# Turning a layer's output with VectorE and device memory instead of TensorE

## The chip, the cores and the metric

The kernel runs on one core of a Trainium2 chip. The core has a matrix engine (TensorE, PE in the profile), VectorE (DVE), ScalarE (ACT), GpSimd (POOL) and SyncE (SP), a scratch memory of 128 partitions (SBUF), an accumulator memory that the matrix engine writes (PSUM, banks of 512 float32 per partition), and 16 transfer engines (DMA) that are fed by the queues of SP, ACT and POOL. The metric is the time of one execution on the device in microseconds; lower is better. All times below are microseconds unless marked otherwise.

## The reference

Two layers, each with three parallel groups of heads on one input projection; then an output projection, a residual and a layer norm. One sequence of 256 positions with 2048 features, all float32.

```python
def layer_norm(x, g, b):
    mu = mean(x); var = mean((x - mu) ** 2)
    return (x - mu) * rsqrt(var + 1e-5) * g + b

def hybrid_layer(x, mem, w_in, ..., w_mem_kv, w_out, ln_g, ln_b):
    h = x @ w_in
    a_q, a_k, a_v, a_z, b_q, b_k, b_v, b_z, b_lr, m_q, m_z = split(h)
    y_a = chunk_band_attention(a_q, a_k, a_v, rel_table)
    y_b = rms_norm(gla_chunk_recurrence(b_q, b_k, b_v, log_sigmoid(b_lr @ gate_w + gate_b) / 16))
    mk, mv = split(mem @ w_mem_kv)
    y_m = memory_attention(m_q, mk, mv)
    y = concatenate([y_a * silu(a_z), y_b * silu(b_z), y_m * silu(m_z)])
    return layer_norm(sqrt(2) * x + y @ w_out, ln_g, ln_b)

for l in range(2):
    h = hybrid_layer(h, mem, w_in[l], ...)
```

## The kernel before

**Products.** Almost all time goes into products of activations with streamed weights. To keep float32 accuracy each operand is split into a high and a low part (`parts`, L114: ScalarE casts the high part, VectorE subtracts it for the low part), and three products are added: high x high, low x high, high x low. Weights come in pieces of 512 KB (`piece`, L128): SP loads a piece into a tile `raw`, ScalarE writes `wh`, VectorE writes `wl`. The pool of these tiles has four buffers of each (`wp`, L79), so the split of a piece waits until TensorE is done with the piece four before it. Two forms of product occur: `as_group` (L272) holds the activations still and streams the weights; `ws_group` (L254) holds the weights still and streams high and low activations side by side (`both`, 512 columns). A `ws_group` has two halves of four pieces; piece number q multiplies quarter q of the features, x[q].

**Between the layers.** The output of layer 0 lies in `res` with positions on partitions (two tiles t of 128 positions, 2048 features each). Layer 1 needs it with features on partitions: operands x[0] to x[3] (`xq`), each [128, 4, 2, 256], which is four blocks of 128 features, high and low part, 256 positions. `norm_between` (L627) normalises `res` in place: ScalarE takes column groups 0 and 2, VectorE 1 and 3. `transposed` (L574) then turns it: for each pair of feature blocks four 128x128 transposes on TensorE into a PSUM bank (L590), then ScalarE and VectorE scale one block each with the norm's gain and bias (L596, L598, per-partition values in `gT`, which L578 and L579 turn out of a row-wise copy), and `parts` splits the result into x. `restored` (L602) applies gain and bias to `res` itself, for the next residual.

**Order.** TensorE and SP run in the order in which the program is written (L49). ScalarE, VectorE and GpSimd are put in order by the scheduler, by data and priority (`tc.high_priority`); the order is fixed when the program is built, and each engine executes its own list in order. Small jobs are generators; `tick` (L52), called after each weight piece, advances one of them by a step, so that each `yield` places the following instructions behind one more piece. `transposed` is started behind group MV (values of the memory) and runs during group MK (keys of the memory, eight pieces); `finish(gens[:1])` (L779) completes it before the first product that reads x, group BQK (L783), which is again a `ws_group` of eight pieces.

**Buffers.** Operands x come from a pool of five (`opp`, L78): four hold the memory's operand during MV and MK, so that x[1] to x[3] take places that MK's second half frees piece by piece. The tag "qk" of pool `hd` has four buffers of 4 KB a partition; they hold q and k of the attention heads (L802, L837).

**GpSimd** computes almost nothing. It issues small loads (gate weights L303, norm vectors L649, L879) and fills constants (L358).

## Time and profile before

| what | value |
|---|---|
| median of 3 runs | 925.61 (925.45 to 925.86) |
| the profiled execution, whole time | 925.59 |
| its span in the profile | 923.8 |
| granted TensorE clock | 0.998 |
| busy: PE, DVE, ACT, POOL | 916.7, 587.9, 498.2, 21.8 |
| moved by transfers | 178.85 MB, mean 194 GB/s |
| group MK on TensorE | 479.38 to 505.54, with the transposes between its pieces |

The profile shows one execution. Its page gives busy times, the span in slices, the transfer queues, the chain of work that ended last, and groups of instructions. Beside the page the trace can be asked for a timeline of one engine, for groups of instructions in a stretch, and for busy times and transfer rates in chosen stretches. Start times count from the start of the span. A line such as `idle before <-releaser` names what ended an engine's wait.

### The profile page before, as it was taken

Reading aid. Unit: us, or ns where it says so; the run is one execution under the profiler, and the core shown is the slowest. Engines: PE = TensorE matmul, PEld = TensorE weight load, DVE = VectorE, ACT = ScalarE, POOL = GpSimd, SP = SyncE. Lnnn points to the kernel's source line nnn. Section 1 sums busy time; section 2 is a strip of 40 time slices with the busy share of each in tenths; the row PEclk is TensorE's granted clock in tenths of the full one; section 3 lists DMA queues with packets and bytes.
Section 4 is the critical chain, followed back from the end, with each engine's and each line's share of the span. In section 5 each row is a group of like instructions: output and inputs, shape, how many; then the busy total and the mean of one; then the engine's idle time right before and its main releaser. Section 6 shows DMA issues by size and latency. Waiting matters only on the chain.

```text
span 923.8 us, 14249 instructions
## 1 busy us (share of the span) xinstructions
PE 916.7 (99%) x5500; PEld 806.5 (87%) x5500; DVE 587.9 (64%) x812; ACT 498.2 (54%) x714; POOL 21.8 (2%) x49
## 2 busy tenths in 40 slices
PE   9999999999999999999999999999999999999997
PEld 7889998998888888888888899889888888888885
DVE  6764478665564666555587666975655555766566
ACT  6644485484454675433566445754744555754350
POOL 1000000000000000000000000000000000110000
PEclk9999999999999999999999999999999999999999
DMA  9955865546554566756675466546555544667652
GB/s 306 334 189 174 306 207 173 161 165 194 183 162 160 171 206 200 219 193 196 227 249 164 150 205 204 193 154 196 170 193 166 164 152 160 199 222 223 198 163 92
DMA packets 71253, 178.85 MB, mean 194 GB/s; under 512 B 7304, under 2 KB 31240, under 8 KB 70928
## 3 DMA queue, kind: packets, MB, share of 16 engines
q1 hardware_dynamic: 69120, 173.30, 57.1%
q0 software_dynamic: 1920, 4.36, 1.8%
q8 instruction: 43, 0.70, 0.3%
q10 hardware_dynamic: 144, 0.26, 0.1%
q14 instruction: 26, 0.21, 0.1%
HBM read 175.77 MB, written 2.10 MB: 193 GB/s over the span
## 4 chain that ended last, share of the span: by engine, by line
PE 98%; DMA 0%; DVE 0%; ACT 0%; SPq 0%; issue 0%
PE acc L93 89%; PE bk L93 8%; PE bk L526 1%; DMA raw<-w 0%; PE bk L561 0%; PE bk L590 0%; PE bk L494 0%; PE bk L393 0%; SPq L177 0%; ACT res L746 0%; ACT wh L116 0%; DVE stats L731 0%; PE bk L340 0%; DVE res L730 0%; DVE res L682 0%
## 5 line engine op out<-in xcount | busy, mean ns | idle before, releaser
L117 DVE TENSOR_TENSOR wl<-raw,wh 128x1024 fp32r<-128x1024 f32 (+3 forms) x321 | 370.0, 1154 | 255.9 <-ACT wh L116 254.9
L116 ACT CAST wh<-raw 128x1024 fp32r<-128x1024 f32 (+3 forms) x321 | 318.7, 994 | 329.9 <-PE acc L93 236.5
L93 PE MATMUL acc<-x,wh 128*128 128x512 f32 x1248 | 398.0, 400 | 0.1
L93 PE MATMUL acc<-wh,x 128*128 128x512 f32 (+2 forms) x1236 | 357.3, 370 | 0.1
L93 PEld LDWEIGHTS acc<-x,wl 128*128 128x128 f32 x1248 | 234.4, 188 | 55.3
L93 PEld LDWEIGHTS acc<-wh,x 128*128 128x128 f32 x1236 | 227.0, 188 | 27.9 <-ACT wh L116 0.6
L93 PE MATMUL acc<-x,wl 128*128 128x256 f32 x1248 | 246.0, 278 | 0.0
L93 PE MATMUL acc<-wl,x 128*128 128x512 f32 (+2 forms) x618 | 228.0, 369 | 0.0
L93 PEld LDWEIGHTS acc<-x,wh 128*128 128x128 f32 x1248 | 192.0, 189 | 1.9 <-ACT wh L116 0.4
L93 PEld LDWEIGHTS acc<-wl,x 128*128 128x128 f32 x618 | 116.0, 188 | 15.0 <-DVE wl L117 0.9
L518 ACT ACTIVATE sc<-sc,mx 128x128 f32<-128x128 f32 (+1 forms) x32 | 14.4, 450 | 20.3 <-DVE mx L516 20.3
L511 DVE SCALAR_TENSOR_TENSOR sc<-bk,bias 128x384 f32<-128x384 f32 x16 | 8.9, 554 | 12.7 <-PE bk L93 12.7
L382 ACT ACTIVATE sc<-sc 128x512 f32<-128x512 f32 x12 | 7.6, 633 | 12.5 <-DVE sc L380 12.5
L117 DVE TENSOR_TENSOR x<-sc,x 128x512 fp32r<-128x512 f32 x20 | 13.3, 684 | 0.7 <-ACT x L116 0.7
L116 ACT CAST x<-raw 128x1024 fp32r<-128x1024 f32 x5 | 5.3, 1053 | 15.3 <-DMA raw<-memT 12.7
L117 DVE TENSOR_TENSOR x<-res,x 128x512 fp32r<-128x512 f32 (+2 forms) x14 | 10.5, 765 | 4.2 <-ACT x L116 4.1
L93 PE MATMUL bk<-qk,qk 128*128 128x128 f32 (+1 forms) x64 | 13.1, 326 | 0.0
L117 DVE TENSOR_TENSOR x<-raw,x 128x1024 fp32r<-128x1024 f32 x5 | 6.1, 1225 | 10.9 <-ACT x L116 10.9
L93 PE MATMUL bk<-sc,asv 128*128 128x256 f32 (+1 forms) x64 | 13.0, 326 | 0.0
L262 DVE SCALAR_TENSOR_TENSOR sc<-acc,sc 128x512 f32<-128x512 f32 x19 | 12.9, 681 | 0.0
L116 ACT CAST x<-sc 128x512 fp32r<-128x512 f32 x20 | 11.8, 615 | 1.3 <-DVE sc L598 1.3
L623 DVE SCALAR_TENSOR_TENSOR res<-res,acc 128x512 f32<-128x512 f32 x15 | 9.7, 684 | 4.2 <-PE acc L93 4.2
(209 smaller groups left out, 567.8 us busy)
## 6 DMA issues: line engine op xcount, KB each, us to landing
raw<-w SPq DMA_DIRECT2D x214, 512.0 KB, 3.9
raw<-w SPq DMA_DIRECT2D x64, 388.0 KB, 3.3
raw<-w SPq DMA_DIRECT2D x83, 256.0 KB, 3.2
bias<-relw SPq DMA_DIRECT2D x16, 192.0 KB, 4.1
res<-xT SPq DMA_DIRECT2D x4, 512.0 KB, 5.0
res<-xn SPq DMA_DIRECT2D x1, 2048.0 KB, 8.2
raw<-memT SPq DMA_DIRECT2D x4, 512.0 KB, 4.3
res<-memT SPq DMA_DIRECT2D x6, 256.0 KB, 6.1
```

The costliest lines, as they stand in the source:

```text
L93: pe.matmul(o, l, r, start=start, stop=stop, skip_group_check=True)
L116: act.copy(hi, src)
L117: dve.tensor_tensor(lo, src, hi.bitcast(F32), op=ALU.subtract)
L262: dve.scalar_tensor_tensor(dst, a, scale, dst, op0=ALU.mult, op1=ALU.add)
L382: act.activation(dd, dd, AF.Abs)
L511: dve.scalar_tensor_tensor(s, pb[:, :384], SCALE, bias[h], op0=ALU.mult, op1=ALU.add)
L518: act.activation(s[:, own[t]], s[:, own[t]], AF.Exp, bias=mx[:, t:t + 1], accum_out=zs[:, t:t + 1])
L526: pe.transpose(pt[:, i * P:(i + 1) * P], s[:, i * P:(i + 1) * P], ident)
L623: dve.scalar_tensor_tensor(r, r, ALPHA, acc, op0=ALU.mult, op1=ALU.add)
```

## The change

TensorE no longer transposes `res`. VectorE turns it in blocks of 32x32 (`dve.transpose`): four instructions, one for each tile t of positions and each half c of a 128-feature block, write tiles `turned` with 32 features on the partitions of each 32-partition stripe. GpSimd writes them into a device-memory tile `blocks` in 16 transfers (64 rows of 2 KB each), which puts the stripes of positions side by side, and loads it again in four transfers of 512 KB (`raws`, 1024 rows of 512 bytes each), one for each quarter of the features. `raws` has features on partitions, eight stripes of 32 positions, and is scaled in place and split into x through a rearranged view. `turned` and `raws` use the four buffers of the tag "qk". The whole quarter q, its load too, is now issued at raised priority. The transfer of the turned blocks is placed over four steps of the generator, the four quarters over four more. A pool in device memory (`drm`) is added. The number of scalings and splits on ScalarE and VectorE stays the same.

```diff
+    drm = enter("drm", 3, space=bass.MemoryType.DRAM)
...
         pe.transpose(pt[:, :P], raw, ident)
         dve.tensor_copy(gT, pt[:, :32])
+        blocks = drm.tile([P, 8, 512], F32, name=nm("blocks"), tag="blocks", bufs=1)
+        turned = {}
+        for t in range(2):
+            for c in range(2):
+                turned[t, c] = hd.tile([P, 2, 16, 32], F32, name=nm("turn"), tag="qk", bufs=4)
+                dve.transpose(turned[t, c].rearrange("p b k j -> p k b j"),
+                              res[:, t].rearrange("p (k b j) -> p k b j", b=4, j=32)[:, :, 2 * c:2 * c + 2])
+        yield 2
+        for t in range(2):
+            for c in range(2):
+                for a in range(4):
+                    pool.dma_start(blocks[c * 64:c * 64 + 64, t * 4 + a].rearrange("(b i) n -> i b n", b=2),
+                                 turned[t, c][a * 32:a * 32 + 32].rearrange("p b k j -> p b (k j)"))
+            yield 1
         for q in range(4):
-            x = operand()
-            hi, lo, _ = x
-            xq.append(x)
-            for j in range(0, 4, 2):
-                pt = bank()
-                y = scratch([P, 2, T])
-                for jj in range(2):
-                    kt = q * 4 + j + jj
-                    for t in range(2):
-                        pe.transpose(pt[:, jj * T + t * P:jj * T + (t + 1) * P], res[:, t, kt * P:(kt + 1) * P], ident)
-                with tc.high_priority(AHEAD // 4):
-                    for jj in range(2):
-                        kt = q * 4 + j + jj
-                        src, g, b = pt[:, jj * T:(jj + 1) * T], gT[:, kt:kt + 1], gT[:, 16 + kt:17 + kt]
-                        if jj == 0:
-                            act.activation(y[:, jj], src, AF.Identity, bias=b, scale=g)
-                        else:
-                            dve.tensor_scalar(y[:, jj], src, g, b, op0=ALU.mult, op1=ALU.add)
-                    parts(hi[:, j:j + 2], lo[:, j:j + 2], y)
-                yield 1
+            with tc.high_priority(AHEAD // 4):
+                raws = hd.tile([P, 8, 128], F32, name=nm("raws"), tag="qk", bufs=4)
+                pool.dma_start(raws, blocks[:, :, q * 128:(q + 1) * 128])
+                x = operand()
+                hi, lo, _ = x
+                xq.append(x)
+                y = raws.rearrange("p g (k j) -> p k g j", j=32)
+                for j in range(4):
+                    kt = q * 4 + j
+                    g, b = gT[:, kt:kt + 1], gT[:, 16 + kt:17 + kt]
+                    if j % 2 == 0:
+                        act.activation(y[:, j], y[:, j], AF.Identity, bias=b, scale=g)
+                    else:
+                        dve.tensor_scalar(y[:, j], y[:, j], g, b, op0=ALU.mult, op1=ALU.add)
+                for j in range(0, 4, 2):
+                    parts(*(z[:, j:j + 2].rearrange("p k (g j) -> p k g j", j=32) for z in (hi, lo)), y[:, j:j + 2])
+            yield 1
```

In the built program the order around the change, beside the instructions that stand in both, is: on VectorE the four turns behind the split of MV's last piece and ahead of the split of MK's first piece; the scaling of quarter 0 behind the split of BQK's second piece; between the first and the second half of x[1]'s low part the scaling of quarter 3. On ScalarE the scaling of quarter 0 stands behind the cast of BQK's second piece, then the cast of the third piece, then the casts of x[0]. On GpSimd the 16 writes come first, then the three loads of gate weights (L303), then the four reads, then the memset of L358.

## The prediction

> **What bounds the kernel now.** The page comes first: its busy times, then the chain that ended last.

> ```profile
> span 923.8 us, 14249 instructions
> ...
> PE 916.7 (99%) x5500; PEld 806.5 (87%) x5500; DVE 587.9 (64%) x812; ACT 498.2 (54%) x714; POOL 21.8 (2%) x49
> ...
> PE 98%; DMA 0%; DVE 0%; ACT 0%; SPq 0%; issue 0%
> ```

> TensorE (PE) is busy for 99% of the span and 98% of the chain of waits is its own. What leaves PE shortens the kernel; what makes PE wait lengthens it one for one. So I read next the chain in order of time between the layers, where the changed code runs (start, length, what).

> ```profile
> 482.32 0.11 PE bk L578
> 482.43 0.44 PE bk L590 x4
> 482.87 2.79 PE acc L93 x16
> 485.66 0.44 PE bk L590 x4
> ...
> 505.11 0.44 PE bk L590 x4
> 505.54 54.46 PE acc L93 x310
> ```

> Eight groups of four transposes (L590) stand in the chain, one after each weight piece. A piece of 16 products takes 2.79. From 505.54 on PE multiplies the turned activations (group BQK), whose first half, four pieces, ends at 505.54 + 4 x 2.79 = 516.7. This is the mark against which I measure: nothing after it is changed, so a shift there is a shift of the end. The profiled execution took 925.59 (span 923.8 and 1.8 around it), 0.02 under the median of 925.61, so shifts are added to 925.6.

> **Removed.** 32 transposes leave PE. One lasts 0.27 by itself, but in the chain four cost 0.44: 8 x 0.44 = 3.5 us. That is the whole of what can be won. L578, the transpose of the norm's vectors, stays.

> **Added: four turns on VectorE.** The order of instructions puts all four directly behind the last weight piece of group MV and ahead of the split of MK's first piece. They wait for the normalised rows. In the timelines (start, length):

> ```profile
> 472.57 2.94 ACT L640 ACTIVATE res<-res,nmr,rstd 128x512 f32<-128x512 f32 x4 [0.61 <-DVE nmr L635]
> ...
> 472.57 1.92 DVE L642 TENSOR_SCALAR res<-res,rstd,nmr 128x512 f32<-128x512 f32 x4
> 474.40 1.22 DVE L117 TENSOR_TENSOR wl<-raw,wh 128x1024 fp32r<-128x1024 f32 x1
> 476.48 3.50 DVE L117 TENSOR_TENSOR wl<-raw,wh 128x1024 fp32r<-128x1024 f32 x3 [0.85 <-ACT wh L116]
> ...
> 479.38 0.62 PE L93 MATMUL acc<-x,wh 128*128 128x512 f32 x2
> 479.83 0.40 PE L93 MATMUL acc<-x,wl 128*128 128x256 f32 x2
> ```

> The rows are normalised at 475.5, and the split begun at 474.40 ends about then. No row shows a 32x32 transpose of 1024 elements a partition. Below stands L642: four of 512 elements in 1.92, so 0.46 each, 0.92 for 1024. Above I put two passes at the split's rate: three splits of 1024 elements take 3.50, so 1.14 each, and twice that is 2.28. I take 1.14, one pass. The turns then end at 475.55 + 4 x 1.14 = 480.1, and MK's first split (before: done at 477.7) at 481.3. PE needs it at 479.83: a stall of 1.5. At 0.92 it is 0.6, at 2.28 it is 6.0. Later MK pieces have 2.79 each against a split of 1.14 and catch up.

> [...]

> **Added: the way through memory.** GpSimd (POOL) issues 16 writes of 131 kB and, when all have landed, four reads of 524 kB, in rows of 512 bytes. What there is to price them: POOL's own issue, landing times, queue totals, and the traffic in the stretches concerned (columns of the last: PE, PEld, DVE, ACT, POOL busy, clock, DMA share, GB/s).

> ```profile
> 482.73 1.48 POOL L303 DMA_DIRECT2D gwraw<-gate_w  x3 [105.14 <-PE bk L578]
> 499.36 0.53 POOL L358 MEMSET sc<- 128x512 f32 x1 [15.16 <-DVE mk L117]
> ...
> out<-res SPq DMA_DIRECT2D x6, 256.0 KB, 2.4
> gb<-ln_g POOLq DMA_DIRECT2D x4, 256.0 KB, 5.7
> gwraw<-gate_w POOLq DMA_DIRECT2D x6, 16.0 KB, 3.4
> gbrow<-gbrow POOLq DMA_DIRECT2D x4, 8.0 KB, 1.7
> ...
> q1 hardware_dynamic: 69120, 173.30, 57.1%
> ...
> 480.00:490.00 10.00, 10.00 (x64) 8.93 (x64) 6.72 (x9) 6.17 (x9) 1.48 (x3) 1.00 0.80 270
> 490.00:500.00 10.00, 10.00 (x63) 8.89 (x62) 8.08 (x12) 7.39 (x13) 0.58 (x2) 1.00 0.49 170
> 500.00:510.00 10.00, 10.00 (x62) 8.85 (x61) 7.88 (x11) 6.86 (x11) 0.06 (x1) 1.00 0.50 167
> ```

> The 16 transfer engines at full share would move 173.30 MB in 0.571 x 923.8 = 527 us, 329 GB/s. Weights need 524 kB in 2.79 us, 188. What is left is 141 GB/s. The writes (2.10 MB) then need 14.9 us from 476.8, when the first turn is done, plus 1.7 to land (the smallest of POOL's rows): 493.4. The reads need as long again, plus 0.5 for the issue (1.48 / 3) and 1.7 to 3.4 to land: the fourth, call it R3, is there at 510.5 to 512.2.

> Early bound: POOL's issue alone limits the writes, 16 x 0.5 = 8 us, 484.8, plus 2.4; the reads have the full 329 GB/s, 6.4 us: R3 = 496. Late bound: the weights take their 270 GB/s of the 480 to 490 stretch for ten microseconds, 59 are left (0.59 MB), then 1.51 MB at 141, 10.7 us: writes landed at 499.2, R3 = 518. I take the middle of the first pair, 511.3, because transfers here are shared with a weight stream that never pauses.

> [...]

> **Moved: the scaling and the splits of x.** Their number stays, eight scalings and eight splits on each of ScalarE and VectorE, but before they were spread over MK's eight pieces, and now they stand bunched behind the reads. For 470 to 520, grouped by line:

> ```profile
> L117 DVE TENSOR_TENSOR wl<-raw,wh 128x1024 fp32r<-128x1024 f32 x18 | 21.9, 1224 | 11.4 <-ACT wh L116 11.4
> L116 ACT CAST wh<-raw 128x1024 fp32r<-128x1024 f32 x18 | 18.6, 1047 | 13.5 <-PE acc L93 13.5
> L117 DVE TENSOR_TENSOR x<-sc,x 128x512 fp32r<-128x512 f32 x8 | 5.4, 684 | 0.7 <-ACT x L116 0.7
> L116 ACT CAST x<-sc 128x512 fp32r<-128x512 f32 x8 | 4.8, 615 | 1.3 <-DVE sc L598 1.3
> L598 DVE TENSOR_SCALAR sc<-bk,gbT 128x256 f32<-128x256 f32 x8 | 4.3, 538 | 0.0
> ```

> The cast of a weight waits for PE to free a buffer, four pieces back. In the new order ScalarE has: scaling of quarter 0, cast of BQK's third piece, then the casts of x0. That piece's buffer is free when MK's seventh piece is done: 479.4 + 7 x 2.79 + 1.5 + 0.1 = 500.5. So x0's high part is there at 500.5 + 1.05 + 0.6 = 502.1, its low part (split of the piece, then of x0) at 503.3, just when PE is ready (503.3). From there VectorE is serial: scaling of quarter 1 (two, 0.9), x0's second half 0.6, scaling of 2 0.9, a weight split 1.2, MK's total 0.6, x1's first half 0.6: 508.1. Next on VectorE is the scaling of quarter 3, which waits for R3, and behind it stands x1's second half. So x1 is complete at max(508.1, R3) + 0.9 + 0.6, and PE has 2.5 pieces left of BQK's half, 7.0: it ends at max(508.1, R3) + 8.5. The rest (x2, x3) comes faster than PE takes it.

> With R3 = 511.3 that is 519.8, 3.1 later than 516.7. With R3 up to 508.1 it is 516.6: the 3.5 won are spent on the stall of 1.5 and the bunching.

> Queued behind the waits: on ScalarE the casts of BQK's pieces and MK's total, which frees the accumulator of BQK's second half; they are late with x, not beyond it. On POOL the writes pass gate_w's three loads (their reader is at 528.9) and the reads pass the memset of 499.36 (its reader comes after 571).

> ```profile
> L349 ACT ACTIVATE sc<-bk,gb x4: 465/468/470, 115.8 to 571.5; 128x256 f32<-128x256 f32 x4
> L305 ACT CAST gw<-gwraw x2: 392/392/393, 73.6 to 528.9; 48x256 fp32r<-48x256 f32 x2
> ```

> Both moves cost nothing unless R3 is beyond 520. SP's queue of weights keeps its order; its loads become slower, which the late bound holds. The q/k buffers were last read in layer 0's mixer and are free.

> **Sum.** -3.5 for the transposes, +1.5 for the stall at MK, +1.9 for the bunched splits, +3.2 for R3 (511.3 - 508.1): +3.1. I round to +3.0: 928.6.

> **The rivals.** First, the transfers are on time (R3 before 508): +0, 925.6. For it speaks that DMA share is 0.5 in the two stretches after 490; against it 0.80 before, and two landings in series. Second, the turn takes two passes (2.28): PE stalls 6.0 at MK, its seventh piece ends at 505.0, 508.1 becomes 512.6, and with R3 no later than that the half ends at 521.1: +4.4, 930.0. For it speaks only that no row prices the instruction. Third, on the other side, faster: x keeps pace with PE, and only the stall at MK is paid: -3.5 + 1.5 = -2.0, 923.6. It needs x1 whole 2.0 before 509.6; against it stands the order on VectorE, where seven instructions lie between x0's and x1's first halves.

> **How the numbers follow.** Late transfers 0.47, on time 0.30, two passes 0.15, faster 0.08. Of a measurement of this kernel 0.2%, 1.85 us, can be told from no change: transfers on time count as the same, late transfers and two passes as slower. The likeliest, late transfers, has its own range from +1.9 to +9.8 (R3 = 518). The whole range takes in on time and stops short of the far ends: 924.0 to 934.5.

> **What would show it.** L590 gone from PE. A gap of PE near 480 of about 1.5 that ends with a split of MK's first piece; no gap says the turn is cheap, 6 says two passes. The last write landed near 493, the fourth read near 511. Gaps of PE between 503 and 513, ended by splits of x. Wrong would be: PE without gaps there (faster), gaps that end with weight loads (the stream starved, which I priced only as a bound), or a shift away from this stage.

## The result and the profile after

| kernel | median | lowest to highest | runs |
|---|---|---|---|
| before | 925.85 | 925.45 to 926.17 | 20 |
| after | 928.58 | 926.20 to 930.89 | 20 |

The changed kernel takes 1.0027 of the time before, 95% interval 1.0020 to 1.0034: 2.7 us slower. Its times are also far more spread, 4.7 us in place of 0.7. The profiled execution took 929.37 (span 927.6), 0.8 above its median.

The page of the changed kernel first: span, busy times, and the engines' shares of the chain that ended last.

```profile
span 927.6 us, 14222 instructions
...
PE 915.8 (99%) x5468; PEld 805.2 (87%) x5468; DVE 590.5 (64%) x816; ACT 498.2 (54%) x714; POOL 34.0 (4%) x69
...
PE 92%; DMA 3%; DVE 2%; ACT 1%; issue 1%; SPq 0%; DVEq 0%; ACTq 0%
```

PE has 32 instructions less, but only 0.9 us less busy time, and its share of the chain falls from 98% to 92%: it now waits for transfers, VectorE and ScalarE. The windows between the layers show where (busy us of PE, PEld, DVE, ACT, POOL, then the clock, the DMA share and GB/s):

```profile
480.00:490.00 10.00, 8.93 (x52) 7.49 (x51) 7.38 (x8) 2.87 (x3) 7.30 (x15) 1.00 0.96 297
490.00:500.00 10.00, 10.00 (x59) 8.71 (x58) 6.85 (x7) 6.26 (x7) 4.22 (x6) 1.00 0.97 340
500.00:510.00 10.00, 6.24 (x33) 5.29 (x32) 5.45 (x11) 6.59 (x11) 0.00 (x0) 0.93 0.97 333
510.00:520.00 10.00, 10.00 (x53) 8.69 (x53) 9.39 (x14) 7.75 (x13) 0.00 (x0) 0.90 0.41 121
```

Before, PE was busy for all of each of these stretches. Now 1.07 is missing near 480 and 3.76 after 500, the transfers are at 0.96 to 0.97 of their capacity for 30 us (0.80, 0.49 and 0.50 before), and from 500 to 520 the mean granted clock is below 1. The chain in order of time names the two waits (start, length, what):

```profile
478.08 2.01 DVE turn L586 x2
...
480.34 1.19 DVE wl L118
...
481.57 2.60 PE acc L94 x14
...
494.79 9.61 DMA raw<-w
...
504.50 1.05 ACT wh L117
...
506.75 0.67 DVE x L118
...
507.56 25.52 PE acc L94 x136
```

The first wait is the forecast one: turns, then the split of MK's piece, then PE. The second is not. It goes back from x[0]'s low part (506.75) to the cast of a weight piece (504.50), BQK's third, and from there to that piece's load, which took 9.61 where the median of such loads is 4.1. The timelines of VectorE, ScalarE and GpSimd add what stood around it:

```profile
475.79 4.62 DVE L586 STREAM_TRANSPOSE turn<-res 128x1024 f32<-128x1024 f32 x4
...
493.13 3.57 POOL L598 DMA_DIRECT2D raws<-blocks  x4 [3.21 <-DMA blocks<-turn]
...
500.01 1.09 ACT L607 ACTIVATE raws<-raws,gbT 128x256 f32<-128x256 f32 x2 [0.89 <-DMA raws<-blocks]
504.50 1.04 ACT L117 CAST wh<-raw 128x1024 fp32r<-128x1024 f32 x1 [3.40 <-DMA raw<-w]
505.46 1.13 ACT L117 CAST x<-raws 128x512 fp32r<-128x512 f32 x2
...
511.55 0.73 DVE L609 TENSOR_SCALAR raws<-raws,gbT 128x256 f32<-128x256 f32 x2
```

The first quarter was scaled from 500.0 to 501.1. Its casts stand behind the weight piece in ScalarE's list and had to wait until 505.46. The last quarter's scaling (511.55) shows no wait: the fourth read was there, having landed at 508.9 (worked out below). The third source of loss is the clock. Three windows of 3.41 us that follow each other show it; the gap of 3.76 begins in the first, at 503.80, and ends in the second, at 507.56:

```profile
501.83:505.24 3.41, 1.97 (x12) 1.54 (x10) 0.00 (x0) 0.73 (x1) 0.00 (x0) 1.00 1.00 345
505.24:508.65 3.41, 1.09 (x6) 0.99 (x7) 3.07 (x6) 3.41 (x7) 0.00 (x0) 1.00 0.93 329
508.65:512.06 3.41, 3.41 (x13) 2.92 (x12) 3.41 (x8) 3.35 (x7) 0.00 (x0) 0.50 0.54 184
```

For 3.41 us PE is busy throughout at a granted clock of 0.50, which is an estimated 1.7 us of work lost: in PE's timeline the products advance by four in 1.28 there (510.60 to 511.88), and by four in 0.70 at full clock (513.38 to 514.08). The stage can be closed with the first product of the next group, in the timelines of the kernel before and of the changed one:

```profile
527.69 0.52 PE L93 MATMUL acc<-wh,x 128*128 128x388 f32 x2
```
```profile
479.88 0.61 PE L94 MATMUL acc<-x,wh 128*128 128x512 f32 x2
...
531.49 0.52 PE L94 MATMUL acc<-wh,x 128*128 128x388 f32 x2
```

From the start of MK (479.38 before, 479.88 after) to there it is 48.31 before and 51.61 after: +3.3. The parts are -3.5 (transposes), +1.1 (turns), +3.8 (gap ahead of BQK), +1.7 (clock): +3.1, so 0.2 is left unexplained. MK itself starts 0.5 later than before. No part above accounts for that; in seven of the experiments below MK starts between 479.47 and 480.00.

### The profile page after: what moved, and what is told of

It is laid out like the page before. It is cut to its first block, busy times and chain, and to the rows that moved or that the text cites. A ratio compares the mean times of both kernels' runs of the same rounds, so it can differ in the third digit from the quotient of the medians.

```text
span 927.6 us, 14222 instructions
## 1 busy us (share of the span) xinstructions
PE 915.8 (99%) x5468; PEld 805.2 (87%) x5468; DVE 590.5 (64%) x816; ACT 498.2 (54%) x714; POOL 34.0 (4%) x69
## 3 DMA queue, kind: packets, MB, share of 16 engines
q1 hardware_dynamic: 69120, 173.30, 58.2%
## 4 chain that ended last, share of the span: by engine, by line
PE 92%; DMA 3%; DVE 2%; ACT 1%; issue 1%; SPq 0%; DVEq 0%; ACTq 0%
PE acc L94 83%; PE bk L94 7%; DMA raw<-memT 2%; DMA raw<-w 2%; DVE wl L118 1%; PE bk L527 1%; ACT wh L117 1%; PE bk L562 0%; ACT x L117 0%; DVE x L118 0%; DVE turn L586 0%; ACT res L652 0%; PE bk L495 0%; PE bk L394 0%; SPq L165 0%
## 5 line engine op out<-in xcount | busy, mean ns | idle before, releaser
L117 ACT CAST wh<-raw 128x1024 fp32r<-128x1024 f32 (+3 forms) x321 | 318.7, 994 | 335.1 <-PE acc L94 227.3
L117 ACT CAST x<-raw 128x1024 fp32r<-128x1024 f32 x5 | 5.3, 1051 | 15.5 <-DMA raw<-memT 12.2
L635 DVE SCALAR_TENSOR_TENSOR res<-res,acc 128x512 f32<-128x512 f32 x15 | 9.7, 683 | 4.5 <-PE acc L94 4.5
L94 PEld LDWEIGHTS bk<-sc,asv 128*128 128x128 f32 x64 | 11.3, 189 | 1.2
L592 POOL DMA_DIRECT2D blocks<-turn x16 | 8.5, 537 | 100.4 <-DVE turn L586 99.2
## 6 DMA issues: line engine op xcount, KB each, us to landing
raw<-w SPq DMA_DIRECT2D x83, 256.0 KB, 3.3
```

The source lines that it names most:

```text
L94: pe.matmul(o, l, r, start=start, stop=stop, skip_group_check=True)
L117: act.copy(hi, src)
L592: pool.dma_start(blocks[c * 64:c * 64 + 64, t * 4 + a].rearrange("(b i) n -> i b n", b=2), turned[t, c][a * 32:a * 32 + 32].rearrange("p b ...
L635: dve.scalar_tensor_tensor(r, r, ALPHA, acc, op0=ALU.mult, op1=ALU.add)
```

## The experiments

All ratios are to the kernel before, run beside them on the same chip, with the 95% interval in brackets. Gaps are PE's waits in the profiled execution.

**1. x[0] ahead of the weight piece.** A copy of one element per partition makes the cast of BQK's third piece wait for x[0], so that ScalarE takes x[0] first.

```diff
 def piece(..., behind=None):
+    if behind is not None:
+        act.copy(hi[:, 0, 0:1], behind)
     parts(hi, lo, raw)
...
-    for i, a, b in ws_group(w512[l, G_BQK], xq):
+    for i, a, b in ws_group(w512[l, G_BQK], xq, {2: 0} if l > 0 else {}):
```

> Theory W: TensorE's gap of 3.8 us ahead of group BQK is the third weight piece of BQK. It landed at 504.5, 9.6 us after its issue, because the reads of the turned blocks share the transfer engines, and its cast stands ahead of the casts of x0 on ScalarE, which have their data from 500.0. Here one instruction of one element makes that cast wait for x0, so x0 goes first. W expects the gap at 503.8 to fall under 1 us, the halved clock behind it to go, a second gap of up to 2 us ahead of x1, and 925 to 927 us. Rival V (the splits bunched on VectorE and the fourth read set the start and end of BQK's first half): x0 comes earlier but x1 to x3 do not, less than 0.7 us is won, 928 to 929 us.

929.85, ratio 1.0041 (1.0028 to 1.0053): above both expectations. PE starts BQK without a gap and then stands still one quarter later, as PE's and VectorE's timelines show:

```profile
508.94 0.73 PE L94 MATMUL acc<-x,wh 128*128 128x512 f32 x2 [3.73 <-DVE x L118]
```
```profile
505.81 0.73 DVE L611 TENSOR_SCALAR raws<-raws,gbT 128x256 f32<-128x256 f32 x2 [1.22 <-DMA raws<-blocks]
506.47 1.22 DVE L118 TENSOR_TENSOR wl<-raw,wh 128x1024 fp32r<-128x1024 f32 x1
507.60 0.68 DVE L265 SCALAR_TENSOR_TENSOR sc<-acc,sc 128x512 f32<-128x512 f32 x1
508.20 0.68 DVE L118 TENSOR_TENSOR x<-raws,x 128x512 fp32r<-128x512 f32 x1
```

3.73 in place of 3.76: the late weight piece was what PE could be seen to wait for, and taking it out of the way does not shorten the wait, because x[1] is late by the same amount. VectorE first waits 1.22 for a read, then takes a scaling, a weight split and MK's total ahead of x[1]'s split, the list that the prediction had written out. The order of the lists is not all that differs: in this execution the first write of a turned block is issued at 475.61, 1.7 sooner than in the changed kernel (477.32), so that the gap near 480 is gone and the reads are issued at 491.51, 1.6 sooner. Even with that lead the wait for x is as long. Behind the gap stand 3.4 us at half clock, as in the changed kernel.

**2. Two turns behind MK's first split.** The third and fourth turn wait for it.

```diff
 turned[t, c] = hd.tile(...)
+if t == 1 and c == 0:
+    dve.tensor_copy(turned[t, c][:, 0, 0, 0:1], latest[0][:, 0, 0:1].bitcast(F32))
```

> The third and fourth turn on VectorE wait for the split of MK's first weight piece. Both theories: the gap of 1.1 us near 480 goes. W: what TensorE wins there it waits longer for the third piece of BQK, whose landing does not depend on TensorE, so 928 to 929 us, a gap of 4.5 to 5 us ahead of BQK. Rival A (the terms are independent and add up): 1.2 us less than the changed kernel, 927.3 us.

928.51, ratio 1.0031 (1.0019 to 1.0043): the same as the changed kernel. The gap near 480 is gone, and most of it comes back later, in gaps of 3.80 and 0.72, together 4.52 against 1.07 + 3.76 = 4.83 in the changed kernel:

```profile
505.91 1.19 PE L94 MATMUL acc<-x,wh 128*128 128x512 f32 x2 [3.80 <-DVE x L118]
511.01 0.73 PE L94 MATMUL acc<-x,wh 128*128 128x512 f32 x2 [0.72 <-DVE x L118]
```

What PE does not lose at MK it loses waiting for x. The edit also issues the reads 1.07 later (494.20), so the run does not part what PE's earlier arrival does from what the later reads do.

**3. Five buffers for `raw`** in place of four, in the changed kernel.

```diff
-raw = wp.tile([P, kp, n], F32, name=nm("raw"), tag="raw")
+raw = wp.tile([P, kp, n], F32, name=nm("raw"), tag="raw", bufs=5)
```

> One more buffer for loaded weight pieces (five instead of four) in the whole kernel, so each load is issued about one piece (2.8 us) earlier. W: the third piece of BQK lands up to 3 us earlier, the gap ahead of BQK falls to 0 to 2 us, 924.5 to 927.5 us. V: x0 is earlier at most by what ScalarE waits, the bunched splits stay, 928 to 929 us.

924.51, ratio 0.9983 (0.9975 to 0.9992): faster than before. One gap of 1.23 is left, and ScalarE waits for a loaded weight piece once, for 1.2, where it waited 11.7 in all in the changed kernel. But the norm also comes 4.4 sooner, and the reads are issued 4.45 earlier:

```profile
488.68 3.57 POOL L598 DMA_DIRECT2D raws<-blocks  x4 [3.27 <-DMA blocks<-turn]
```

**4. The kernel before, with the traffic alone.** Turns, writes and reads are added to the kernel before; what the reads bring is not used.

> The kernel before, transposes on TensorE kept, with the four turns, the 16 writes and the four reads added; nothing reads what they load. W: the weights' loads become slow here too, but the four pieces in hand cover it, as nothing of x stands behind them; TensorE waits only for the turns near 480, 1.2 us: 926.5 to 927.5 us. Rival S (the starved weight stream stops TensorE by itself): gaps ended by weight splits between 485 and 510 too, 928.5 us or more.

926.89, ratio 1.0011 (1.0003 to 1.0020). PE's timeline has one gap, that of the turns:

```profile
481.76 0.51 PE L94 MATMUL acc<-x,wl 128*128 128x256 f32 x2 [1.57 <-DVE wl L118]
```

ScalarE does wait 6.2 us for weight pieces in this kernel, but PE is not held up: its split pieces are a stock that covers it. Here the slower weight stream costs PE nothing; in the changed kernel x stands behind it.

**5. The kernel before with five buffers**, the control of the third.

> The kernel before, with five buffers instead of four for the raw tiles (weight pieces and the other loads that share that name), nothing of the change in it: the control for the changed kernel with five. If the 4 us that the fifth buffer gave the changed kernel came because its weight pieces were late beside the turned blocks, the kernel before gains nothing, having had no wait of ScalarE for a weight piece in this stretch: 925.9, ratio 0.999 to 1.001. If the fifth buffer lets the whole chain of an earlier stage start sooner whatever the turn is done with, the kernel before gains too: 922 to 924.5, ratio 0.996 to 0.9985, and then the turn through device memory is still about 1 to 3 us slower than the transposes at equal buffers.

926.16, ratio 1.0003 (0.9994 to 1.0011): no gain, though here too the norm comes sooner with the fifth buffer, by 3.8. VectorE's first row of the norm, at 472.57 in the prediction's rows, is now:

```profile
468.75 1.00 DVE L642 TENSOR_SCALAR res<-res,rstd,nmr 128x512 f32<-128x512 f32 x2
```

A head start is worth something only to the changed kernel, which needs it for the detour.

**6. Both lists put in order.** The first experiment's edit, and VectorE's scaling of the third and fourth quarter waits for the low part of the quarter before.

```diff
+if q > 1:
+    own = small([P, 2, 4], f"gq{q}")
+    dve.tensor_copy(own[:, 0, 0:1], xq[q - 1][1][:, 1, 0:1].bitcast(F32))
+    dve.tensor_copy(own, gq)
+    gq = own
```

> The changed kernel with two waits added by tiny copies: ScalarE's cast of BQK's third weight piece waits for the first quarter of x (as in the first run), and VectorE's scaling of the third and the fourth quarter waits for the low part of the quarter before it, so that the scalings no longer stand ahead of splits that TensorE waits for. Theory (two limits of nearly the same time, the late weight piece and the list on VectorE): with both out of the way the gap of 3.7 us ahead of or in group BQK falls to 0 to 1.5 us and the half clock behind it goes: 925.0 to 926.5, ratio 0.999 to 1.001. Rival (the reads' landing is the third limit, right behind): the quarters come as the reads land, the gap stays above 2.5 us, perhaps in parts between the quarters: 927.5 to 929.5.

933.87, ratio 1.0085 (1.0071 to 1.0100): above both expectations, by 7 and by 4 us. PE's timeline:

```profile
504.24 0.70 PE L94 MATMUL acc<-x,wh 128*128 128x512 f32 x2 [0.28 <-DVE x L118]
510.43 1.22 PE L94 MATMUL acc<-x,wh 128*128 128x512 f32 x2 [3.16 <-DVE x L118]
517.68 1.22 PE L94 MATMUL acc<-x,wh 128*128 128x512 f32 x2 [2.76 <-DVE x L118]
```

The last gap, 2.76 ahead of x[2], comes with the edit. The scaling is half ScalarE's, and its gain comes from the tile that VectorE now writes late, so the third quarter is handed from one engine to the other: ScalarE waits 1.52 for that tile and scales at 513.02, and then a weight piece goes ahead of x[2]'s casts. The gap ahead of x[1], 3.16, has another source. No scaling of a later quarter stands ahead of x[1]'s split any more, but a weight split and MK's total do (VectorE, 507.95 to 509.77). So the scalings alone were not the fault. Three windows at half clock (10.25 us) add an estimated 5.1.

**7 and 8. Five buffers with the scalings in order, without and with x[0] first.**

> The changed kernel with five raw buffers and VectorE's scaling of the third and the fourth quarter behind the low part of the quarter before it. If the one gap left with five buffers (1.2 us at x1's split, and some 0.7 in small ones) is VectorE's list, it goes: 923.0 to 923.9, 0.5 to 1.5 under the kernel with five buffers alone (924.5). If it is the reads' landing, the time stays at 924.5 within 0.4.

> The same with both added waits: five raw buffers, the first quarter of x ahead of BQK's third weight piece on ScalarE, and VectorE's scalings in order. If the weight piece is still part of what is left with five buffers, this is 0.3 to 1 us faster than the kernel with the scalings in order alone; if it is not, the two agree within 0.4 us, since TensorE runs the weight pieces in any order before x has come.

926.59, ratio 1.0006 (0.9997 to 1.0015), and 929.68, ratio 1.0040 (1.0026 to 1.0054): both slower than five buffers alone (924.51) and outside what was expected of them. As in the sixth, ScalarE waits for the late gain (1.6 and 2.3), and new gaps of 1.17 and 2.57 appear behind. With x[0] first as well, PE stands still for 4.43 in place of 2.82 and two windows at half clock follow, where the two kernels were to agree or the second to be faster. The run does not show the reason given for that: TensorE's order is that of the program, and with x[0] first it stands still for 1.86 and for 2.57 until x is split (509.18 and 516.11), the first time with three weight pieces split by 507.93. The added waits cost time in all three of these kernels.

**9. Writes on two queues.** Every second write is issued by ScalarE, to have the reads start sooner.

```diff
-pool.dma_start(blocks[c * 64:...], ...)
+(act if a % 2 else pool).dma_start(blocks[c * 64:...], ...)
```

> The changed kernel with every second write of the turned blocks issued by ScalarE in place of GpSimd (8 of 16 each), everything else as changed. GpSimd takes 0.53 us to issue one, so the sixteenth write is issued some 4 us earlier, and the reads behind it, and the scheduler puts x's scalings and splits further forward. Theory (TensorE stands still because x's quarters come some 4 us too late for the room that the weight splits leave on VectorE): 924.5 to 926.5, the gap ahead of BQK under 1.5 us. Rival (the slow weight stream is what counts: the loads are as slow beside the same transfers, only at another moment): 928 to 930, a wait of ScalarE for a weight piece of over 3 us still stands ahead of x's casts. A third way: ScalarE's issues and the waits for turned blocks hold up the casts of weight pieces around 476 to 482, with a gap of over 1.5 us there.

926.86, ratio 1.0017 (1.0008 to 1.0026). The premise did not come true: ScalarE's writes stand in its list behind casts that wait, the last two are issued from 482.56 on, and the reads start at 493.13, exactly as in the changed kernel. So this run says nothing of earlier reads. What did change is the order that the scheduler gave x and the weights: the gaps after 500 are 1.45, 0.53 and 1.17 in place of one of 3.76, ended by weight pieces that stand behind x. The gap near 480 is 1.59. Together that is 4.74, as much as the changed kernel's 4.83, and the clock stays at 1.00 through 500 to 520.

**10. Two queues and five buffers.**

> The kernel with five raw buffers and the writes on two queues. If the 1.2 us gap left with five buffers comes from x being late, it goes and the time is 923.0 to 924.0. If x put forward now waits for the reads at the head of ScalarE's list, with weight casts behind it, the time is 925 to 928.

923.00, ratio 0.9972 (0.9962 to 0.9982), the fastest of all and faster than before. GpSimd's timeline and the windows:

```profile
486.80 3.57 POOL L598 DMA_DIRECT2D raws<-blocks  x4 [2.17 <-DMA raw<-w]
```
```profile
480.00:490.00 10.00, 10.00 (x59) 8.75 (x58) 6.44 (x7) 4.88 (x5) 4.68 (x7) 1.00 0.97 359
490.00:500.00 10.00, 10.00 (x60) 8.72 (x58) 5.15 (x10) 6.26 (x11) 1.02 (x3) 1.00 0.99 323
500.00:510.00 10.00, 10.00 (x60) 8.70 (x59) 10.00 (x16) 10.00 (x16) 0.00 (x0) 1.00 0.58 194
510.00:520.00 10.00, 10.00 (x59) 8.72 (x58) 8.77 (x11) 5.05 (x7) 0.00 (x0) 1.00 0.76 236
```

The reads are issued 6.3 earlier than in the changed kernel and PE does not stand still in this stage, although the transfers are just as full until 500 and VectorE and ScalarE are busy for all of 500 to 510. The span is 3.2 under that of the kernel before: the 3.5 of the transposes, nearly whole. Experiment 9 is its control: the same two queues, without the earlier reads, left as much standing still as the changed kernel has.

**11. Five buffers, turns held back**, so that the reads are late again while the weights keep their buffer: the second experiment's copy, but ahead of the first turn (`t == 0 and c == 0`).

> Five raw buffers, but the four turns held back behind a split of the next group's weights, so that writes and reads come again about as late as with four buffers (reads issued near 493 us in place of 488.7), while the weight pieces keep their fifth buffer. If the fifth buffer helped by its head start alone, the gain goes: 927 to 929.5. If it helped because weight pieces loaded beside the transfers are no longer late, the gain stays: 924 to 925.5.

926.90, ratio 1.0013 (1.0004 to 1.0022), just below the range given for the head start alone. Its GpSimd and PE timelines, and what ScalarE waited for from 470 to 530 (us in total, times, longest):

```profile
491.75 3.57 POOL L603 DMA_DIRECT2D raws<-blocks  x4 [3.10 <-DMA blocks<-turn]
```
```profile
505.29 1.19 PE L94 MATMUL acc<-x,wh 128*128 128x512 f32 x2 [3.14 <-DVE x L118]
```
```profile
ACT wh L117 <- PE acc L94: 22.7, 14, 1.9
```

No wait of ScalarE for a weight's load is left, and the gap of 3.14 is there all the same. The fifth buffer's 4 us were mostly the head start. Reads issued 3.1 later than in the third experiment cost 2.4 us; what is left of its lead over the changed kernel (1.7 between the medians) may be the reads' remaining 1.4 of lead or the weights' buffer, which this run does not part.

**12. The kernel before with a stall put in.** ScalarE casts one weight piece of BQK eleven times; no turned blocks move.

```diff
+    for _ in range(again):
+        act.copy(hi, raw)
     parts(hi, lo, raw)
```

> The kernel before, nothing of the change in it, with a stall put in: ScalarE casts the third weight piece of BQK's second half eleven times in place of once (ten more casts of about 1.05 us each, ScalarE having some 6 us of lead there), so that TensorE stands still for 3 to 6 us, the length G to be read from the profile, with no transfer of turned blocks anywhere. Theory (a gap of TensorE of over some 2.5 us is itself followed by about 3 us at half the granted clock): the windows right behind the gap show 0.50 and the time is G plus 1.3 to 2 us above the kernel before. Rival (the half clock belongs to the changed kernel's transfers and splits running together): the granted clock stays at 1.00 behind the gap and the time is G above, within 0.5.

934.35, ratio 1.0089 (1.0075 to 1.0103): 8.4 us more. PE's timeline and the windows:

```profile
528.98 1.22 PE L93 MATMUL acc<-x,wh 128*128 128x512 f32 x2 [5.95 <-ACT wh L116]
```
```profile
521.63:525.04 3.41, 1.41 (x9) 1.03 (x7) 0.00 (x0) 3.35 (x5) 0.00 (x0) 1.00 0.00 0
525.04:535.28 10.24, 6.26 (x18) 4.86 (x19) 5.41 (x6) 4.58 (x5) 0.00 (x0) 0.50 0.34 109
```

The half clock comes without any of the change's transfers, so it belongs to the standing still. It lasts 6.3 us beyond the gap, longer than expected (3), and half of that, an estimated 3.1, is lost work: 5.95 + 3.1 = 9.1, where the profiled execution (935.65) is 9.7 above the kernel before and the median 8.4.

Put together, by the time at which the reads are issued:

| kernel | reads issued | gap near 480 | gaps of PE after 500 | half clock | median |
|---|---|---|---|---|---|
| 10 | 486.80 | none | none | none | 923.00 |
| 3 | 488.68 | none | 1.23 | none | 924.51 |
| 1 | 491.51 | none | 3.73 | 3.4 | 929.85 |
| 11 | 491.75 | none | 3.14 | 3.4 | 926.90 |
| changed kernel | 493.13 | 1.07 | 3.76 | 3.4 | 928.58 |
| 9 | 493.13 | 1.59 | 3.15 | none | 926.86 |
| 2 | 494.20 | none | 4.52 | 3.4 | 928.51 |

PE's standing still, both columns together, grows by and large with the time of the reads, whatever is named as its releaser: from nothing at 486.80 to between 4.5 and 4.8 from 493.13 on. One window of 3.41 at half clock adds an estimated 1.7. Experiments 6, 7 and 8 are left out, since their added waits make gaps of their own (7.15, 2.82 and 4.43 in all; the reads of 6 and 7 are issued from 493.75 and 488.89). The medians follow less closely: single executions of the kernels with half clock differ by 2 to 5 us, and 1 and 11, with reads 0.24 apart, have medians 2.95 apart, which is not explained.

## Why the prediction came out, step by step

**The transposes, -3.5.** Right. With all waits gone (experiment 10) the span is 3.2 shorter than before.

**One pass for a turn, stall of 1.5 at MK.** Right in kind and size: four turns in 4.62 are 1.15 each (1.14 forecast), the stall is 1.07, and 1.57 where the turns run in the kernel before. That rules out the rival of two passes. To add it to the later terms was doubtful: experiment 2 took the stall away and won nothing, since most of it came back as a longer wait for x, in a run whose reads were later too.

**Writes landed at 493.4.** Right: the reads, which wait for the last write, were issued from 493.13 on.

**The fourth read, +3.2.** This term failed. The tile `raws` in the changed kernel shows when the reads were issued and how long they took to land:

```profile
L598 POOL DMA_DIRECT2D raws<-blocks x4: 882/892/929, 493.1 to 495.8; - x4
...
DMA to landing us min/median/max: 6.8/9.9/13.1
```

The shortest is the first, the longest the last: they landed from 499.9 to 508.9, about 3.0 apart. The fourth was forecast for 511.3. By the prediction's own max(508.1, R3), 508.9 is worth 0.8 in place of 3.2, and in the run nothing waited for it: VectorE came to the fourth quarter only at 511.55. The step that was wrong is the sharing of the transfers. The reads were given the 141 GB/s that the weights leave; 524 kB every 3.0 us is an estimated 175, and as all transfers together ran at 333 to 340 GB/s, about 160 was left for weights that need 188. So the reads were early and the weights late.

**x[0] at 502 to 503, PE ready at 503.3 without a gap.** Failed. The cast of BQK's third piece was forecast for 500.5, when its buffer is free, and ran at 504.50, when its data had come. The prediction had named gaps behind weight loads as a sign against it, and priced the starved stream only as a bound of the reads. By experiment 1 the failure cost little or nothing of its own: with x[0] on time PE waits 3.73 for x[1], though all the reads came 1.6 sooner.

**The list on VectorE, +1.9.** Right in place, too small. Once the weight piece is out of the way (experiment 1), x[1]'s first half is done at 508.9 (508.1 forecast) and PE waits for it, 3.73. In that list VectorE also waits 1.22 for a read, the third quarter's, which the sum did not have.

**The clock.** Not in the prediction at all: an estimated 1.7, from 3.41 us at 0.50.

The sum is where it was forecast, +3.1, because two terms that were not foreseen as they came (3.8 ahead of BQK, 1.7 of clock) stand in the place of two that were (1.9 and 3.2). As far as the number goes, that is luck. It shows in the single runs: the seven of the changed kernel's 20 with the highest mean clock (0.998) have a median of 926.57, only 0.7 above the kernel before, less than the 1.85 that the prediction takes as no change. The forecast size is reached by the other thirteen, which have a lower clock. The kind of the mechanism, x too late through device memory and then bunched on VectorE, is shown by experiments 3, 10 and 11, with 9 as a control; the term that was to carry most of it, the fourth read, is not. Whether reads in longer rows than 512 bytes would land sooner was not tried.

**The rivals.** On time (925.6): its condition was the fourth read before 508. At 508.9 it missed that narrowly; but no engine waited for that read, and the kernel was slower for other reasons. Two passes: ruled out by the length of the turns. Faster, x keeps pace: not here, but in experiment 10, where the reads come 6.3 us sooner.

**How long a transfer took.** From issue to landing, at the median of the changed kernel's writes and reads (the last column, in us):

```profile
blocks<-turn POOLq DMA_DIRECT2D x16, 128.0 KB, 5.2
raws<-blocks POOLq DMA_DIRECT2D x4, 512.0 KB, 9.9
```

## What to carry to other kernels

When work is taken off a full engine and sent round through memory, ask first how long ahead of its use the result must be started: here the detour was worth its 3 us once its reads began 6 us sooner (experiment 10: 3.1 under the kernel before), and cost 2.7 as written. The releaser that the profile names for a gap need not be worth anything; take it away before you believe it, since a second wait of the same length may stand right behind (experiment 1: 3.73 in place of 3.76). A gap in a matrix engine that was never idle before can cost more than its length, through the clock: here an estimated 1.7 us more behind a gap of 3.76, and 3.1 more behind one of 5.95 (experiment 12).

## What was not expected of the hardware

```profile
507.19:510.60 3.41, 1.55 (x10) 1.23 (x9) 3.41 (x5) 1.64 (x3) 0.00 (x0) 1.00 0.93 311
510.60:514.00 3.40, 2.94 (x11) 2.25 (x9) 1.23 (x5) 1.94 (x3) 0.00 (x0) 0.50 0.52 175
```

So the 3.41 us ahead of a stretch need not be idle: here PE was busy for 45% of them.

**The spread of the times.** Of the changed kernel's 20 runs, the seven with a mean clock of 0.998 took 926.20 to 927.22, the thirteen with 0.995 to 0.997 took 927.79 to 930.89. One stretch of 3.41 us at 0.50 lowers the mean of 927 us by 0.0018, so the two groups fit runs without and with such a stretch. Only profiled executions show the stretch itself; for the other runs this is inferred. It is not the whole of the spread: the two groups' medians, 926.57 and 929.20, lie 2.6 apart and not 1.7, and experiment 9's profiled execution took 928.33, 1.5 above its median, with the granted clock at 1.00 in every stretch from 470 to 530.
